# A decoder layer on one Trainium2 core: FFN output sums carried in PSUM by ScalarE, accumulators copied out by ScalarE, and two-chunk plans in blocks 3 and 5

## The chip, the core and the metric

One core of a Trainium2 chip runs the whole kernel. Its engines work side by side, each through a queue of its own in order: TensorE (PE: matmuls, and PEld, its weight loads), VectorE (DVE), ScalarE (ACT), GpSimd (POOL) and SyncE (SP, which here issues the loads of weights). They wait for each other by semaphores. SBUF holds the working data; the matmuls accumulate in PSUM, eight banks of 128 partitions x 512 floats. The metric is the device time of one execution in microseconds (us), the median of several.

## The reference

A decoder layer over 256 tokens of width 2048, all in float32: an FFN, a token mixer (sparse attention beside a recurrence), and a second FFN, each with a residual and a layer norm. The change touches the two FFNs alone:

```python
def swiglu(h, w_in, w_out):
    a, b = jnp.split(h @ w_in, 2, axis=-1)
    return (jax.nn.silu(a) * b) @ w_out

h = layer_norm(DN_ALPHA * h + 0.5 * swiglu(h, ffn1_w_in[l], ffn1_w_out[l]), ln1_g[l], ln1_b[l])
...
h = layer_norm(DN_ALPHA * h + 0.5 * swiglu(h, ffn2_w_in[l], ffn2_w_out[l]), ln3_g[l], ln3_b[l])
```

with 2048 inputs, 2 x 5632 hidden columns and 2048 outputs.

## The kernel before

**Precision.** Each float32 operand is split into a high and a low part, both of a type that TensorE multiplies in one pass, and a product is three matmuls (`three`: high by high, high by low, low by high; L564 to L566). For the weights ScalarE makes the high part (`wh`, L192) and VectorE subtracts it from the weight for the low one (`wl`, L193), piece by piece, up to 1024 columns each. This splitting is most of the two engines' work in the FFNs. Pieces are split four ahead of their use (`AHEAD`) into five pairs of buffers and loaded another four ahead.

**Blocks.** An FFN is 22 blocks. A block computes 256 hidden columns of each of a and b (with the tokens' 256 columns as the moving side, so hidden channels lie on partitions) in two PSUM accumulators `c[0]` and `c[1]`, called `mm` in the trace. There are two such banks in all (`CB`, bufs 2), so the first product of a block into `mm` can't start until the block before has been read out of both. The sum over the 2048 inputs is cut into four chunks. A chunk is computed plainly (form "c": two pieces of 1024 columns, 24 matmuls of 512 columns), or by a scheme with seven products in place of eight on half-size operands (forms `p1q3`, `p2`, `q5p7`, `q4p6`: 42 matmuls of 256 columns). The seven-product form saves TensorE work and needs sums of weights, which VectorE makes (L165, L169, L172) before they are split. Four of its partial sums, p1, p6, p7 and q5, stand in two further banks `e` (`bp` in the trace), and the gate adds them to the accumulators. `layer_plans` says which blocks have how many seven-product chunks (`block_plan(3, 4)`: three chunks, four fills).

**Fills.** The second matmul of the FFN runs in the blocks as fills (form "o"): the hidden blocks are grouped (`SEGS`: 2 blocks, then 4 x 5), and while one group is computed, the outputs of the group before are formed, 4 column ranges `nb` of 512, in two banks `ob` (`OB`, bufs 2), one for each half of the tokens. A range of groups 1 to 4 (`s` is counted from 0) sums over four blocks and is finished with the four fills of one block; in the plan of blocks 6 to 21 two fills come first in the block and two at its end. Group 0 is summed in blocks 2 to 5 with two fills each. At the end of each range VectorE adds half of the bank to the running output `Y` in SBUF (`y_add`, L699). The last group is done after the blocks by `out_product`, which uses `y_add` on its own path.

**The gate.** After a block's last product `gate` puts p1, p6, p7, q5 and the accumulators together into z (SBUF, 4 x 256 columns, one buffer), takes the silu of a, multiplies with b (L871), and 7 pieces later (`LAG_T`) TensorE transposes z back (L877); ScalarE and VectorE split the result into `g` (L689, L690) for the fills. In the code before, ScalarE only copies p1 to z (L859) and takes the silu (L866); VectorE does the adds (L860, L861, L862) and, last, L865 twice: z plus `c[t]`, which reads the accumulators.

**Order.** PE, SP and POOL run in the order in which the code is written. ACT and DVE are put in order by a scheduler at build time, which is free to move an instruction among others where data allows.

Of the kernel before, what the change touches and what calls it, by code (L numbers as in the profile page):

```python
# [8 lines left out]
F32 = mybir.dt.float32  # L9
F32R = mybir.dt.float32r  # L10
I32 = mybir.dt.int32
AF = mybir.ActivationFunctionType
OP = mybir.AluOpType
AX = mybir.AxisListType.X

P = 128
S = 256
# [36 lines left out]
Z_BUFS = 1  # L54
# [12 lines left out]
def block_plan(fast, fills, lead=2):  # L67

    chunks = {0: (), 2: (1, 3), 3: (1, 2, 3)}[fast]
    plain = [("c", k) for q in range(4) if q not in chunks for k in (4 * q, 4 * q + 2)]
    forms = [(f, q) for q in chunks for f in FORMS]
    rest = ["o"] * fills
    plan = [(rest.pop(), 0) for _ in range(min(lead, fills))] + [plain.pop(0)]
    slow = []
    while plain or rest:
        for which in (rest, plain) if lead else (plain, rest):
            if which:  # L80
                p = which.pop(0)
                slow.append((p, 0) if p == "o" else p)
    if not forms:
        return plan + slow
    step = len(forms) / (len(slow) + 1)
    n = 0
    for i, f in enumerate(forms):
        plan.append(f)
        if len(slow) > n and i + 1 >= (n + 1) * step:
            plan.append(slow[n])  # L90
            n += 1
    return plan


def layer_plans(first):
    return ([block_plan(0, 0), block_plan(first, 0)] + [block_plan(2, 2, 0), block_plan(3, 2)] * 2
            + [block_plan(3, 4)] * 16)


# [162 lines left out]
def tile_layer(ctx, tc, x_fm, x_tm, pos, f1a, f1o, wA, wki, wB, lru, wab, wrb, wo, f2a, f2o,  # L262
# [5 lines left out]
    V, A, T, G = nc.vector, nc.scalar, nc.tensor, nc.gpsimd  # L268
    count = [0]

    def name(s):
        count[0] += 1
        return f"{s}{count[0]}"
# [4 lines left out]
    def UHL(s):  # L278
        return U(s, F32R).rearrange("p (a t) -> p a t", a=2)

    def T1(s="t"):
        return pool.tile([P, S], F32, name=name(s), tag="t", bufs=T_BUFS)
# [10 lines left out]
    def OB():  # L293
        return psum.tile([P, 512], F32, name=name("ob"), tag="ob", bufs=2)
# [7 lines left out]
    def BP():  # L302
        return psum.tile([P, 512], F32, name=name("bp"), tag="bp", bufs=4)
# [35 lines left out]
    for i in range(NR + LAG):  # L339
        if i < NR:  # L340
            plain([wB[RX + i], wB[RG + i]])
        if i >= LAG:
            g, c = divmod(i - LAG, TPG)
# [8 lines left out]
    W = Weights(nc, pool, pieces, bg.step)  # L352
# [165 lines left out]
    Y = [[None] * 4 for _ in range(2)]  # L518
# [43 lines left out]
    def three(ps, xh, xl, w, start, stop, seeded=False):  # L562
        h, l = (v.rearrange("p (a h c) -> p a c h", h=2, c=P) for v in w)
        T.matmul(ps, xh, h, start=start, stop=False, skip_group_check=seeded)  # L564
        T.matmul(ps, xh, l, start=False, stop=False, skip_group_check=seeded)  # L565
        T.matmul(ps, xl, h, start=False, stop=stop, skip_group_check=seeded)  # L566

    def tokens(ps, x, t, w, start, stop, seeded=False):
        three(ps, x[:, 0, t * P:(t + 1) * P], x[:, 1, t * P:(t + 1) * P], w, start, stop, seeded)
# [118 lines left out]
    def split(dst, f):  # L688
        A.activation(dst[:, 0], f, AF.Copy)  # L689
        V.tensor_tensor(dst[:, 1], f, dst[:, 0], op=OP.subtract)  # L690
# [3 lines left out]
    def new_stats():  # L694
        stats["st"] = [pool.tile([P, 24], F32, name=name("st"), tag="st", bufs=2) for _ in range(2)]

    def y_add(ps, nb, stat, t):
        y = Y[t][nb]
        V.scalar_tensor_tensor(y, ps[t], 0.5, y, op0=OP.mult, op1=OP.add)  # L699
        if stat:  # L700
            V.bn_stats(stats["st"][t][:, nb * 6:nb * 6 + 6], y)
# [149 lines left out]
    def ffn(x, forms, ln, plans):  # L851
        def gate(c, e, g, i, lag):

            z = W.fast_pool.tile([P, 4 * S], F32, name=name("z"), tag="z", bufs=Z_BUFS)
            z4 = z.rearrange("p (j c) -> p j c", j=4)
            a, b = z4[:, 0:4:2], z4[:, 1:4:2]
            if e:
                p1, p6, p7, q5 = e[0][:, :S], e[0][:, S:], e[1][:, :S], e[1][:, S:]
                A.activation(z4[:, 0], p1, AF.Copy)  # L859
                V.tensor_tensor(z4[:, 1], z4[:, 0], p6, op=OP.add)  # L860
                V.tensor_tensor(z4[:, 2], z4[:, 1], p7, op=OP.add)  # L861
                V.tensor_tensor(b, q5[:, None, :].to_broadcast([P, 2, S]), z4[:, 1:3], op=OP.subtract)  # L862
                for t in range(2):
                    zt = z[:, t * 512:(t + 1) * 512]
                    V.tensor_tensor(zt, zt, c[t], op=OP.add)  # L865
                A.activation(a, a, AF.Silu)  # L866
            else:
                for t in range(2):
                    A.activation(z4[:, 2 * t], c[t][:, :S], AF.Silu)
                    A.activation(z4[:, 2 * t + 1], c[t][:, S:], AF.Copy)  # L870
            V.tensor_tensor(a, a, b, op=OP.mult)  # L871
            for _ in range(lag):
                yield
            ps = BP()
            for k in range(2):
                for t in range(2):
                    T.transpose(ps[:, k * S + t * P:k * S + (t + 1) * P], z[:, t * 512 + k * P:t * 512 + (k + 1) * P], ident)  # L877
            for k in range(2):
                hl = UHL("g")
                split(hl, ps[:, k * S:(k + 1) * S])  # L880
                g[i + k] = hl

        g = [[None] * (2 * (b1 - b0)) for b0, b1 in SEGS]
        fills = deque(FILLS)
        open_ps = []

        def seed():
            s, nb, _ = fills[0]
            open_ps[:] = OB(), OB()

        def fill():
            if not open_ps:
                seed()
            s, nb, k0 = fills.popleft()
            for k in (k0, k0 + 1):
                w = W.unit(512)
                for t in range(2):
                    tokens(open_ps[t], g[s][k], t, w, k == 0, k == len(g[s]) - 1)
            if k0 + 2 == len(g[s]):
                for t in range(2):  # L900
                    y_add(open_ps, nb, False, t)
                if fills:
                    seed()

        for s, (b0, b1) in enumerate(SEGS):
            for n in range(b0, b1):
                c, e = blockF(x, forms, plans[n], fill)
                task = gate(c, e, g[s], 2 * (n - b0), LAG_T[n == NBK - 1])
                next(task)
                bg.add("gate", task)  # L910
        new_stats()
        ln.prepare()
        if not ln.last:
            bg.add("main", later(consts(), W.last.ins))
        out_product(g[-1], ln)
# [189 lines left out]
    for j in range(NK):  # L1105
        s = sumB(blockB(hs))
# [6 lines left out]
    for j in range(NK):  # L1113
        s = sumB(blockB(ya))
# [40 lines left out]
    for j in range(NR + LAG):  # L1155
        if j < NR:
            s = block3(hs)
# [12 lines left out]
        if j >= LAG:  # L1170
            i = j - LAG
            g, c = divmod(i, TPG)
# [6 lines left out]
            r, t = T1(), T1()  # L1179
# [11 lines left out]
    for j in range(NK):  # L1191
        s = sumB(blockB(hs))
# [8 lines left out]
    for j in range(NK):  # L1201
        s = sumB(blockB(yr))
# [91 lines left out]
```

## Time and profile before

| what | us |
|---|---|
| median of 3 runs (2427.35 to 2430.88) | 2427.51 |
| profiled execution, its own time | 2428.93 |
| span of that execution in the trace | 2427.0 |
| PE busy (share of span) | 2313.7 (95%) |
| PEld busy | 2104.2 (87%) |
| DVE busy | 2038.9 (84%) |
| ACT busy | 1410.3 (58%) |
| mean granted TensorE clock | 0.987 of full |

The first FFN lasts from the start to some 710 us, the mixer to some 1690, the second FFN to the end. A busy share is an average over these stages; what a stage is worth is read from the stage. In rows of the timeline the columns are start, duration, engine, line of the code, operation, output<-inputs, shape, and in brackets the idle time before and what ended it. In groups (by line) they are busy time and mean of one in ns, then the idle time in front. Rows of waits read: engine and line that waited, for which engine and line; total, times, longest. Matmuls overlap, so the distance from one start to the next is a matmul's cost, not its duration. "issue" is time in which the engine waited for nothing that the profile shows.

### The profile page before, as it was taken

To read this page: it belongs to the slowest core of one execution; us is meant where nothing else is said; L and a number is where in the kernel's file an instruction comes from. 1 tells how busy PE (TensorE), PEld (TensorE's weight loads), DVE (VectorE), ACT (ScalarE), POOL (GpSimd) and SP (SyncE) were. 2 spreads that over 40 slices of the span, in tenths; PEclk is the share of its full clock that TensorE was granted. 3 is DMA by queue.
4 is the path that set the end of the run, shared out by engine and by line. 5 is a ranking of instruction groups with operands and counts; after the bars stand their busy time and mean duration, and the time that the engine had idled before them with its cause. 6 is when DMAs were issued, how large, how long until landed. Compare 5 with 4: busy or idle time off the path is not lost.

```text
span 2427.0 us, 37550 instructions
## 1 busy us (share of the span) xinstructions
PE 2313.7 (95%) x14592; PEld 2104.2 (87%) x14592; DVE 2038.9 (84%) x2835; ACT 1410.3 (58%) x1931; POOL 25.9 (1%) x58
## 2 busy tenths in 40 slices
PE   7889999999989999999999999999989999999997
PEld 6788888888878888888999988888878888888886
DVE  7889999999987776655788875666989999999996
ACT  6555655655646555544688874444755655655652
POOL 0000000000000000000000000000000000000001
PEclk9999999999999999999999999999999999999998
DMA  7445555555556554455555555556645555556563
GB/s 285 167 171 195 208 198 197 193 193 194 197 178 213 180 177 156 148 183 189 176 190 183 182 198 185 187 192 194 213 172 203 193 189 199 197 207 222 208 215 111
DMA packets 112770, 463.41 MB, mean 191 GB/s; under 512 B 12720, under 2 KB 12720, under 8 KB 97488
## 3 DMA queue, kind: packets, MB, share of 16 engines
q1 hardware_dynamic: 110592, 454.61, 53.6%
q0 software_dynamic: 2000, 6.41, 1.0%
q8 instruction: 114, 1.87, 0.3%
q14 instruction: 64, 0.52, 0.1%
HBM read 458.87 MB, written 2.10 MB: 190 GB/s over the span
## 4 chain that ended last, share of the span: by engine, by line
PE 83%; DVE 8%; issue 5%; ACT 3%; DMA 1%; POOL 0%; DVEq 0%; SPq 0%; ACTq 0%; POOLq 0%
PE mm L564 8%; PE mm L566 8%; PE mm L565 8%; PE ob L564 6%; PE ob L566 6%; PE ob L565 6%; PE mm L553 5%; PE ob L553 5%; PE bp L566 4%; PE bp L565 4%; PE bp L564 4%; DVE wl L193 3%; PE mm L554 3%; PE ob L554 3%; ACT wh L192 2%
## 5 line engine op out<-in xcount | busy, mean ns | idle before, releaser
L193 DVE TENSOR_TENSOR wl<-raw,wh 128x1024 fp32r<-128x1024 f32 (+3 forms) x630 | 752.7, 1202 | 300.8 <-ACT wh L192 300.3
L192 ACT ACTIVATE wh<-raw 128x1024 fp32r<-128x1024 f32 (+3 forms) x630 | 652.8, 1045 | 502.7 <-issue 146.3
L192 ACT ACTIVATE wh<-rf 128x1024 fp32r<-128x1024 f32 x354 | 320.5, 916 | 181.6 <-PE mm L566 143.9
L193 DVE TENSOR_TENSOR wl<-rf,wh 128x1024 fp32r<-128x1024 f32 x354 | 365.9, 1041 | 10.6 <-ACT wh L192 7.0
L564 PE MATMUL ob<-wh,g 128*128 128x512 f32 x640 | 246.6, 385 | 1.0 <-ACT g L689 1.0
L566 PE MATMUL ob<-wh,g 128*128 128x512 f32 x640 | 243.2, 380 | 0.6 <-DVE g L690 0.6
L565 PE MATMUL ob<-wl,g 128*128 128x512 f32 x640 | 243.1, 380 | 0.0
L564 PE MATMUL mm<-wh,hs 128*128 128x512 f32 (+1 forms) x600 | 207.5, 346 | 30.0 <-ACT wh L192 15.7
L192 ACT ACTIVATE wh<-ws 128x1024 fp32r<-128x1024 f32 x118 | 125.3, 1061 | 146.2 <-issue 62.9
L566 PE MATMUL mm<-wh,hs 128*128 128x512 f32 (+1 forms) x600 | 205.0, 342 | 1.7 <-DVE hs L755 1.4
L565 PE MATMUL mm<-wl,hs 128*128 128x512 f32 (+1 forms) x600 | 204.6, 341 | 0.0
L564 PE MATMUL mm<-wh,xs 128*128 128x256 f32 (+1 forms) x464 | 156.6, 338 | 46.2 <-ACT wh L192 24.5
L565 PE MATMUL bp<-wl,sh 128*128 128x256 f32 x708 | 195.1, 276 | 1.6 <-DVE wl L193 1.6
L566 PE MATMUL bp<-wh,sl 128*128 128x256 f32 x708 | 194.7, 275 | 0.0
L564 PE MATMUL bp<-wh,sh 128*128 128x256 f32 x708 | 194.6, 275 | 0.0
L564 PEld LDWEIGHTS mm<-wh,hs 128*128 128x128 f32 x600 | 114.6, 191 | 48.3 <-ACT wh L192 22.6
L565 PE MATMUL mm<-wl,xs 128*128 128x256 f32 (+1 forms) x464 | 154.2, 332 | 1.3 <-DVE wl L193 1.3
L193 DVE TENSOR_TENSOR wl<-ws,wh 128x1024 fp32r<-128x1024 f32 x118 | 144.0, 1221 | 13.1 <-ACT wh L192 13.1
L566 PE MATMUL mm<-wh,xs 128*128 128x256 f32 (+1 forms) x464 | 154.2, 332 | 0.0
L165 DVE TENSOR_TENSOR ws<-rf 128x1024 f32<-128x1024 f32 x118 | 143.8, 1219 | 0.0
L564 PEld LDWEIGHTS mm<-wh,xs 128*128 128x128 f32 x464 | 90.4, 195 | 60.6 <-ACT wh L192 30.5
L565 PEld LDWEIGHTS bp<-wl,sh 128*128 128x128 f32 x708 | 135.8, 192 | 3.6 <-DVE wl L193 2.4
(301 smaller groups left out, 5795.3 us busy)
## 6 DMA issues: line engine op xcount, KB each, us to landing
raw<-wB SPq DMA_DIRECT2D x144, 512.0 KB, 3.6
rf<-f1a SPq DMA_DIRECT2D x60, 1024.0 KB, 4.8
rf<-f2a SPq DMA_DIRECT2D x58, 1024.0 KB, 4.9
raw<-f1o SPq DMA_DIRECT2D x88, 512.0 KB, 5.7
raw<-f2o SPq DMA_DIRECT2D x88, 512.0 KB, 5.7
raw<-wA SPq DMA_DIRECT2D x64, 512.0 KB, 3.6
raw<-f2a SPq DMA_DIRECT2D x60, 512.0 KB, 4.9
raw<-f1a SPq DMA_DIRECT2D x56, 512.0 KB, 5.7
```

Of the source, the lines that this page charges most:

```text
L165: v.tensor_tensor(t, b[:, 0:4:3], b[:, 1:2].to_broadcast([P, 2, 2, 256]), op=OP.add)
L192: nc.scalar.activation(hp, src, AF.Copy)
L193: self.last = nc.vector.tensor_tensor(lp, src, hp, op=OP.subtract)
L553: T.matmul(ps, w[0], x.rearrange("p a t -> p (a t)"), start=first, stop=False)
L554: T.matmul(ps[:, :S], w[1], x[:, 0], start=False, stop=last)
L564: T.matmul(ps, xh, h, start=start, stop=False, skip_group_check=seeded)
L565: T.matmul(ps, xh, l, start=False, stop=False, skip_group_check=seeded)
L566: T.matmul(ps, xl, h, start=False, stop=stop, skip_group_check=seeded)
```

## The change

Three edits, all in the FFNs:

1. `layer_plans`: blocks 3 and 5 have two seven-product chunks in place of three, as blocks 2 and 4 have.
2. `gate`: z has 6 x 256 columns. ScalarE copies both accumulators and p1 into z (new L860 twice, L861) at the block's end, so that the accumulators are read by ScalarE alone. VectorE then adds p1, p6, p7, q5 and the copies (L862 to L867: four of 256 columns and two of 512) from what is now mostly SBUF; silu is L868, the product L873.
3. `seed` and `fill`: for the groups s = 1 to 4 ScalarE writes 2 x Y into the bank `ob` before the first fill (L893), the fills' matmuls add to it from the first one on (start false), and at the range's end ScalarE copies the bank out to Y with scale 0.5 (L906). VectorE's two `y_add` of such a range go. Group 0 keeps them.

```diff
--- before.py
+++ after.py
@@ -93,7 +93,7 @@
 
 
 def layer_plans(first):
-    return ([block_plan(0, 0), block_plan(first, 0)] + [block_plan(2, 2, 0), block_plan(3, 2)] * 2
+    return ([block_plan(0, 0), block_plan(first, 0)] + [block_plan(2, 2, 0), block_plan(2, 2)] * 2
             + [block_plan(3, 4)] * 16)
 
 
@@ -851,23 +851,25 @@
     def ffn(x, forms, ln, plans):
         def gate(c, e, g, i, lag):
 
-            z = W.fast_pool.tile([P, 4 * S], F32, name=name("z"), tag="z", bufs=Z_BUFS)
-            z4 = z.rearrange("p (j c) -> p j c", j=4)
-            a, b = z4[:, 0:4:2], z4[:, 1:4:2]
+            z = W.fast_pool.tile([P, 6 * S], F32, name=name("z"), tag="z", bufs=Z_BUFS)
+            z6 = z.rearrange("p (j c) -> p j c", j=6)
+            a, b = z6[:, 0:4:2], z6[:, 1:4:2]
             if e:
                 p1, p6, p7, q5 = e[0][:, :S], e[0][:, S:], e[1][:, :S], e[1][:, S:]
-                A.activation(z4[:, 0], p1, AF.Copy)
-                V.tensor_tensor(z4[:, 1], z4[:, 0], p6, op=OP.add)
-                V.tensor_tensor(z4[:, 2], z4[:, 1], p7, op=OP.add)
-                V.tensor_tensor(b, q5[:, None, :].to_broadcast([P, 2, S]), z4[:, 1:3], op=OP.subtract)
                 for t in range(2):
-                    zt = z[:, t * 512:(t + 1) * 512]
-                    V.tensor_tensor(zt, zt, c[t], op=OP.add)
+                    A.activation(z6[:, 2 * t:5 + t:4 - t], c[t].rearrange("p (j c) -> p j c", j=2), AF.Copy)
+                A.activation(z6[:, 1], p1, AF.Copy)
+                V.tensor_tensor(z6[:, 0], z6[:, 0], p1, op=OP.add)
+                V.tensor_tensor(z6[:, 1], z6[:, 1], p6, op=OP.add)
+                V.tensor_tensor(z6[:, 3], z6[:, 1], p7, op=OP.add)
+                V.tensor_tensor(z6[:, 2], z6[:, 2], z6[:, 3], op=OP.add)
+                V.tensor_tensor(b, q5[:, None, :].to_broadcast([P, 2, S]), b, op=OP.subtract)
+                V.tensor_tensor(b, b, z6[:, 4:6], op=OP.add)
                 A.activation(a, a, AF.Silu)
             else:
                 for t in range(2):
-                    A.activation(z4[:, 2 * t], c[t][:, :S], AF.Silu)
-                    A.activation(z4[:, 2 * t + 1], c[t][:, S:], AF.Copy)
+                    A.activation(z6[:, 2 * t], c[t][:, :S], AF.Silu)
+                    A.activation(z6[:, 2 * t + 1], c[t][:, S:], AF.Copy)
             V.tensor_tensor(a, a, b, op=OP.mult)
             for _ in range(lag):
                 yield
@@ -887,6 +889,8 @@
         def seed():
             s, nb, _ = fills[0]
             open_ps[:] = OB(), OB()
+            for t in range(2 if s else 0):
+                A.activation(open_ps[t], Y[t][nb], AF.Copy, scale=2.0)
 
         def fill():
             if not open_ps:
@@ -895,10 +899,13 @@
             for k in (k0, k0 + 1):
                 w = W.unit(512)
                 for t in range(2):
-                    tokens(open_ps[t], g[s][k], t, w, k == 0, k == len(g[s]) - 1)
+                    tokens(open_ps[t], g[s][k], t, w, not s and k == 0, k == len(g[s]) - 1, bool(s))
             if k0 + 2 == len(g[s]):
                 for t in range(2):
-                    y_add(open_ps, nb, False, t)
+                    if s:
+                        A.activation(Y[t][nb], open_ps[t], AF.Copy, scale=0.5)
+                    else:
+                        y_add(open_ps, nb, False, t)
                 if fills:
                     seed()
```

What a scheduler made of it is seen in the built programs' orders, in three places. In these rows each line is the code line, operation, output<-inputs with buffer numbers, and shape.

First, ScalarE at the end of a late block (6 to 21). Before, the last splits of the old block (`wh` of `raw` and `rf`) stand directly ahead of the gate's copy of p1:

```order
L192 ACTIVATE wh_3335<-raw_3261 128x1024
L192 ACTIVATE wh_3355<-raw_3279 128x1024
L192 ACTIVATE wh_3367<-raw_3298 128x1024
L192 ACTIVATE wh_3383<-rf_3317 128x1024
L859 ACTIVATE z_3401<-bp_3138 128x256
L192 ACTIVATE wh_3412<-rf_3317 128x512
L192 ACTIVATE wh_3429<-ws_3385 128x1024
L192 ACTIVATE wh_3450<-raw_3365 128x1024
```

With the change:

```order
L192 ACTIVATE wh_3316<-raw_3242 128x1024
L906 ACTIVATE y_318<-ob_3001 128x512
L893 ACTIVATE ob_3334<-y_349 128x512
L906 ACTIVATE y_320<-ob_3002 128x512
L192 ACTIVATE wh_3338<-raw_3260 128x1024
L893 ACTIVATE ob_3335<-y_351 128x512
L192 ACTIVATE wh_3350<-raw_3279 128x1024
L192 ACTIVATE wh_3366<-rf_3298 128x1024
L860 ACTIVATE z_3384<-mm_3099 128x2x256
L860 ACTIVATE z_3384<-mm_3100 128x2x256
L861 ACTIVATE z_3384<-bp_3119 128x256
L192 ACTIVATE wh_3398<-rf_3298 128x512
```

Two copies out of `ob` (L906) and the first one into the next pair of banks (L893) now stand ahead of the split `wh_3338` (`wh_3355` before), the second one behind it. The two accumulator copies (L860) stand after the old block's last splits, ahead of the copy of p1, which is L861 now.

Second, VectorE at the same place. Before (two L699 stand three rows above the first of these):

```order
L193 TENSOR_TENSOR wl_3368<-raw_3298,wh_3367 128x1024
L193 TENSOR_TENSOR wl_3384<-rf_3317,wh_3383 128x1024
L860 TENSOR_TENSOR z_3401<-z_3401,bp_3138 128x256
L169 TENSOR_TENSOR rf_3317<-ws_3385,rf_3317 128x2x256
L861 TENSOR_TENSOR z_3401<-z_3401,bp_3139 128x256
L193 TENSOR_TENSOR wl_3413<-rf_3317,wh_3412 128x512
L862 TENSOR_TENSOR z_3401<-bp_3139,z_3401 128x2x256
L172 TENSOR_TENSOR rf_3317<-rf_3317 128x2x256
L865 TENSOR_TENSOR z_3401<-z_3401,mm_3118 128x512
L865 TENSOR_TENSOR z_3401<-z_3401,mm_3119 128x512
L193 TENSOR_TENSOR wl_3430<-ws_3385,wh_3429 128x1024
L871 TENSOR_TENSOR z_3401<-z_3401 128x2x256
```

With the change, from the gate's first add on:

```order
L862 TENSOR_TENSOR z_3384<-z_3384,bp_3119 128x256
L863 TENSOR_TENSOR z_3384<-z_3384,bp_3119 128x256
L193 TENSOR_TENSOR wl_3399<-rf_3298,wh_3398 128x512
L864 TENSOR_TENSOR z_3384<-z_3384,bp_3120 128x256
L172 TENSOR_TENSOR rf_3298<-rf_3298 128x2x256
L865 TENSOR_TENSOR z_3384<-z_3384 128x256
L193 TENSOR_TENSOR wl_3416<-ws_3368,wh_3415 128x1024
L866 TENSOR_TENSOR z_3384<-bp_3120,z_3384 128x2x256
L193 TENSOR_TENSOR wl_3437<-raw_3348,wh_3436 128x1024
L867 TENSOR_TENSOR z_3384<-z_3384 128x2x256
L165 TENSOR_TENSOR ws_3472<-rf_3396 128x1024
L873 TENSOR_TENSOR z_3384<-z_3384 128x2x256
```

L699 is gone, and the two reads of `mm` (L865) with it; the adds of the gate are spread over more rows, and the product (L871 before, L873 now) stands behind three splits and sums of 1024 columns instead of one.

Third, ScalarE at the boundary from block 3 to block 4, where no fill's bank changes hands in a way that ScalarE sees (group 0). Before:

```order
L192 ACTIVATE wh_1141<-raw_1073 128x1024
L192 ACTIVATE wh_1159<-rf_1087 128x1024
L192 ACTIVATE wh_1171<-rf_1087 128x512
L192 ACTIVATE wh_1190<-raw_1123 128x1024
L859 ACTIVATE z_1206<-bp_980 128x256
L192 ACTIVATE wh_1219<-ws_1161 128x1024
L866 ACTIVATE z_1206<-z_1206 128x2x256
```

With the change:

```order
L192 ACTIVATE wh_1119<-raw_1036 128x1024
L192 ACTIVATE wh_1131<-rf_1066 128x1024
L860 ACTIVATE z_1184<-mm_969 128x2x256
L192 ACTIVATE wh_1149<-rf_1066 128x512
L192 ACTIVATE wh_1168<-raw_1101 128x1024
L860 ACTIVATE z_1184<-mm_970 128x2x256
L861 ACTIVATE z_1184<-bp_988 128x256
L192 ACTIVATE wh_1200<-ws_1133 128x1024
```

The copy of `c[0]` stands ahead of two of the last splits of the block, that of `c[1]` and of p1 behind them.

## The prediction

> **What bounds the kernel now.** I read the page first, its busy shares by slice.
>
> ```profile
> PE   7889999999989999999999999999989999999997
> DVE  7889999999987776655788875666989999999996
> ```
>
> Both FFNs (left third, right third) keep TensorE and VectorE above 90% together; between them TensorE alone is full. The diff touches the FFNs only. Next, windows over their blocks: FFN1's blocks 2 to 7, cut where TensorE begins each.
>
> ```profile
> 58.60:93.02 34.42, 26.90 (x161) 24.58 (x161) 26.80 (x33) 15.65 (x18) 0.00 (x0) 0.90 0.46 164
> 93.02:118.65 25.63, 25.29 (x180) 23.62 (x178) 25.52 (x33) 15.42 (x20) 0.00 (x0) 1.00 0.46 169
> 118.65:154.52 35.87, 26.84 (x161) 24.51 (x161) 28.31 (x34) 16.18 (x19) 0.00 (x0) 0.90 0.48 173
> 154.52:179.99 25.47, 25.13 (x180) 23.66 (x179) 25.36 (x33) 15.25 (x19) 0.00 (x0) 1.00 0.47 170
> 179.99:214.68 34.69, 31.97 (x205) 29.15 (x203) 32.73 (x39) 19.75 (x24) 0.00 (x0) 0.95 0.58 211
> 214.68:246.09 31.41, 30.29 (x205) 28.01 (x204) 30.96 (x38) 18.75 (x22) 0.00 (x0) 1.00 0.53 200
> ```
>
> Columns: window, length, busy of PE, PEld, DVE, ACT, POOL, granted clock. Blocks 2, 4 and 6 are some 9, 10 and 4 us longer than their PE time at full clock; every later block takes 31.41 us, of which DVE fills 30.96. The waits of TensorE name the releaser:
>
> ```profile
> PE mm L564 <- DVE z L865: 40.5, 8, 9.0
> PE mm L564 <- ACT wh L192: 40.2, 31, 6.7
> PE bp L565 <- DVE wl L193: 2.2, 5, 0.6
> ```
>
> The timeline of PE places the long ones, each at the first product of a block into the accumulators `mm`:
>
> ```profile
> 66.12 0.77 PE L564 MATMUL mm<-wh,xs 128*128 128x512 f32 x1 [7.52 <-DVE z L865]
> 127.68 0.77 PE L564 MATMUL mm<-wh,xs 128*128 128x512 f32 x1 [9.03 <-DVE z L865]
> 188.05 0.45 PE L564 MATMUL mm<-wh,xs 128*128 128x512 f32 x1 [2.72 <-DVE z L865]
> 690.74 0.76 PE L564 MATMUL mm<-wh,g 128*128 128x512 f32 x1 [4.78 <-DVE z L865]
> 1803.23 0.77 PE L564 MATMUL mm<-wh,hs 128*128 128x512 f32 x1 [9.03 <-DVE z L865]
> 1863.79 0.45 PE L564 MATMUL mm<-wh,hs 128*128 128x512 f32 x1 [2.71 <-DVE z L865]
> 2366.59 0.77 PE L564 MATMUL mm<-wh,g 128*128 128x512 f32 x1 [3.46 <-DVE z L865]
> ```
>
> The 31 waits on "ACT wh" are the same wait in the late blocks. A late boundary (the last fill's end at 368.37, the next block's `mm` at 378.20), rows of PE, ACT, DVE:
>
> ```profile
> 368.37 0.27 PE L564 MATMUL mm<-wh,xs 128*128 128x256 f32 x1
> 369.04 0.28 PE L564 MATMUL bp<-wh,sh 128*128 128x256 f32 x1
> 376.69 0.38 PE L566 MATMUL ob<-wh,g 128*128 128x512 f32 x1
> 378.20 0.45 PE L564 MATMUL mm<-wh,xs 128*128 128x512 f32 x1 [1.13 <-ACT wh L192]
> 384.21 0.27 PE L877 MATMUL bp<-ident,z 128*128 128x128 f32 x1
> ...
> 368.62 2.04 ACT L192 ACTIVATE wh<-raw 128x1024 fp32r<-128x1024 f32 x2 [1.43 <-issue]
> ...
> 369.69 1.28 DVE L699 SCALAR_TENSOR_TENSOR y<-ob,y 128x512 f32<-128x512 f32 x2
> 370.89 2.35 DVE L193 TENSOR_TENSOR wl<-raw,wh 128x1024 fp32r<-128x1024 f32 x2
> 373.16 1.22 DVE L193 TENSOR_TENSOR wl<-rf,wh 128x1024 fp32r<-128x1024 f32 x1
> 374.30 0.41 DVE L860 TENSOR_TENSOR z<-z,bp 128x256 f32<-128x256 f32 x1
> 374.63 0.68 DVE L169 TENSOR_TENSOR rf<-ws,rf 128x512 f32<-128x512 f32 x1
> 377.37 1.28 DVE L865 TENSOR_TENSOR z<-z,mm 128x512 f32<-128x512 f32 x2
> 378.56 1.22 DVE L193 TENSOR_TENSOR wl<-ws,wh 128x1024 fp32r<-128x1024 f32 x1
> ```
>
> The first L865 ends at 378.05, 0.15 before the matmul, exactly the distance at 188.05 and 690.74; the ACT row is a coincidence. So one thing holds TensorE at every block's end: `mm` is freed by the last adds of a chain on a VectorE that is full.
>
> **Late blocks (6 to 21).** DVE instructions follow each other at 1.14 us for 1024 columns (370.89 to 373.16 for two), 0.60 for 512 and 0.33 for 256 (374.30 to 374.63). Removed: two L699, 1.20. The gate chain was L860, L861, L862, L865 twice (0.33 + 0.33 + 3 x 0.60); it becomes four of 256 and two of 512 (4 x 0.33 + 2 x 0.60), 0.1 more. DVE: 30.96 - 1.2 + 0.1 = 29.85 us. PE without its wait: a matmul of 512 follows the last after 0.215, so 376.69 + 0.215 against 378.20 loses 1.3, and the first piece lasts 2.66 for 2.59 (rows below): 31.41 - 1.36 = 30.05 us. Both are now within 0.2 us, so what is late next decides.
>
> That is ScalarE's queue at the block's end. It gets six copies there: two sums out, two seeds in, two accumulators. Behind them wait three `wh`, then their `wl` on DVE, then the gate. Prices:
>
> ```profile
> L977 ACT ACTIVATE stg<-mm 128x512 f32<-128x512 f32 x8 | 4.8, 597 | 4.7 <-PE mm L566 4.7
> L859 ACT ACTIVATE z<-bp 128x256 f32<-128x256 f32 x41 | 15.6, 382 | 10.2 <-PE bp L566 10.2
> 40.64 1.14 ACT L530 ACTIVATE y<-y 128x512 f32<-128x512 f32 x2
> ```
>
> A PSUM copy of 512 takes 0.60, and the next starts after 0.52 (1.14 for two); a `wh` of 1024 after 0.96. No row shows ScalarE writing PSUM: between a 256 copy (0.38) and a 1024 one (1.06) I take 0.60, that of the same size. The page "ScalarE: Activation LUTs" of the Trainium skill (What ACT_TABLE_LOAD costs; Step-by-step) gives 186 ns + 0.833 ns a column, an estimate of 0.61 us for 512, and calls PSUM the faster destination; by it the sum stays.
>
> From T0 = 368.37 in the old block's terms: sum out at 0.25 (as `wh` at 368.62), the seed waits for its end, 0.9, second sum 1.4, `wh` 1.95, seed 2.9, two `wh` 3.4 and 4.4, accumulators 5.35 and 5.9, `p1` 6.4, done 6.8. DVE: first gate add 6.85, then by its new order 256, 512, 256, 512, 256, 1024, 512, 1024, 512, 1024 columns, and the product: 3 x 0.33 + 0.33 + 4 x 0.60 + 3 x 1.14 = 7.1, starts 14.0, ends 14.7. TensorE wants z for its transposes at 384.21 - 368.37 - 1.36 = 14.5. So **a new wait, on the product (now L873), of about 0.35 us** takes the old one's place: 30.4 us a block. The seeds are in at 3.4; the fill that needs the second one gets there at 3.35 (six-matmul steps of 0.67, rows 368.37 and 369.04, five of them) + 0.65: covered by 0.5. `wl` for the next fill is also ready some 0.2 early. If this cover goes, TensorE stalls by the excess. Gain 1.0 us over 2 x 15 boundaries: **-30 us**; ends: 0 (chain 1 us longer, with seeds at 1.06) and -41 (no wait, 30.05).
>
> **Early blocks.** A long wait costs twice: after it matmuls run slowly.
>
> ```profile
> 66.12:70.25 4.13, 4.13 (x12) 3.43 (x13) 1.74 (x3) 0.63 (x1) 0.00 (x0) 0.64 0.00 0
> 188.05:192.41 4.36, 4.36 (x13) 3.46 (x14) 4.36 (x5) 0.63 (x1) 0.00 (x0) 0.61 0.00 0
> 359.17:361.76 2.59, 2.59 (x14) 2.27 (x13) 2.59 (x3) 1.59 (x2) 0.00 (x0) 1.00 1.03 413
> 378.20:380.86 2.66, 2.66 (x12) 2.31 (x13) 2.66 (x4) 0.64 (x1) 0.00 (x0) 1.00 0.00 0
> ```
>
> The same 12 matmuls take 4.13 and 4.36 after waits of 7.5 and 2.7 us (granted clock 0.64, 0.61), 2.66 after 1.1, and 2.59 undisturbed: 1.5 to 1.8 us on top. The Trainium skill ("TensorE: Matmul & The Clock Gate", What's actually happening) has the clock halved only after an idle window of about 3.4 us; by it the 2.7 us waits would cost nothing more and the sum would be 3.5 us smaller, but the row at 188.05 shows the loss, so it stays.
>
> Accumulator 0 is complete before the last seven-product pieces, accumulator 1 after half of the last one; ScalarE copies both within about 1.2 us of that. Left over: 0.5 us at 66.12, where a `wh` stands between the copies and c1's comes at 59.6, and 0.2 at the two long ones. Then: FFN1 block 1 to 2, 7.5 + 1.5 - 0.5 = 8.5; block 3 to 4 in both FFNs, 2 x (9.0 + 1.5 - 0.2) = 20.6; block 5 to 6 in both, 2 x (2.7 + 1.8) = 9.0. Blocks 3 and 5 give up a seven-product chunk. PE pays 24 matmuls of 512 at 0.215 for 42 of 256 at 0.112 (0.67/6): 0.5 each, 1.9 in all, against which some of the five stalls on `wl` (2.2 us, third row of the waits) go with the VectorE work; I call that even. On DVE such a chunk costs four `wl`, 3 x 1.14 + 0.60, and three sums, 1.14 + 2 x 0.60: 6.4 us. As a plain chunk it costs two `wl`, 2.3 us, so 4.1 less. In the pair of blocks of the third and fourth window DVE has 28.31 + 25.36 = 53.7 to do, PE 26.84 + 25.13 less 1.5 of slow restart, 50.5; with the change it is 49.6 beside 51. DVE then keeps up where PE no longer stands still, and that is what makes the rest of this term real. If it doesn't, half of this term returns. The loads change from one of 1 MB to two of 0.5 MB for such a chunk, same bytes, issued four pieces ahead, DMA 0.46 to 0.58 busy: nothing. Sum **-38 us**.
>
> **Ends of the FFNs.** 690.74 and 2366.59 are the same wait. FFN2: 3.5 + 1.5 (as at 66.12) - 0.4 = 4.6. FFN1: there DVE has constants to compute behind it and is full until the output products, so I count only 2 us, the sums out and adds that it loses. **-6.6 us.**
>
> **Sum.** The profiled execution took 2428.9 us (span 2427.0), 1.4 over the median. 2428.9 - 30 - 38 - 6.6 = **2354.3**; with the block model good to no better than a microsecond I say 2355.
>
> **Rivals.**
> A: ScalarE's chain eats the late gain (each seed near 1.06, or the copies reached 1 us late). It is for this that six copies wait for a fill's end ahead of three `wh`; against it, ACT is busy 18.75 of 31.41. 2428.9 - 44 (the other two terms) = 2385.
> B: no new wait; two engines at 99%. The margins of 0.2 to 0.5 speak against it. 2428.9 - 41 - 38 - 6.6 = 2343.
> C: late blocks as said, but DVE lags in blocks 2 to 6 and half of that term returns: 2354.3 + 19 = 2373.
> D: the change doesn't do what it says, since ScalarE, in order, reaches the accumulators no sooner than VectorE did: the early waits stay and DVE's savings alone count, some 10 us: 2419. The order above speaks against it.
> E: slower. The cycle fill, sum out, seed, `wh`, `wl`, gate, transposes, next fill sets the block. It costs 30.4 with copies of 0.60. The early and end gains are 44 us; 30 blocks must lose more than that, 1.5 us each over 31.41, so 32.9: the chain 2.5 us longer, six copies at about 1.02 or both seeds at 1.85. From there on it is slower; at 1.1 each it is 2428.9 - 44 + 30 x 2 = 2445. Every PSUM row of ACT is at 0.60 or less.
>
> **Chances.** Forecast 0.50 (2348 to 2362), A 0.17, B 0.13, C 0.12, D 0.04, E 0.04. The range takes in A to C with the seed's bounds: 2340 to 2387. A measurement of this kernel tells about 0.2% (5 us) from no change. Faster 0.95, same 0.01, slower 0.04.
>
> **What would show it.** In the changed profile: no PE wait on DVE's z adds into `mm`; clock 1.00 through 66 to 215 us; late blocks of 30.4 us with DVE still above 97% and a short wait at the transposes on L873; seed rows (ACT, ob<-y) near 0.60; TensorE's first `ob` matmul not waiting. Wrong if blocks stay at 31.4 with DVE idle on "ACT wh" behind the copies (A), or if PE waits on `wl` in blocks 2 to 6 (C).

## The result, and the profile after

The changed kernel takes 2334.08 us (median of 4, 2333.59 to 2336.85) against 2427.43 (median of 4): a ratio of 0.9615, with a 95% interval of 0.9598 to 0.9631. That is faster by 93 us, where 72 were forecast, and below the range (2340 to 2387). The profiled execution took 2333.59, 95.3 less than the one before.

The page of the changed kernel, its busy shares by slice (40 slices of the span):

```profile
PE   8999999999999999999999999999999999999996
DVE  8999999999987786555788875665999999999997
PEclk9999999999999999999999999999999999999999
```

TensorE is now above 90% in every slice but the first and the last. Windows over blocks 2 to 5 of FFN1 and over one late block, columns as in the prediction (length, then busy of PE, PEld, DVE, ACT, POOL, granted clock):

```profile
57.00:171.00 114.00, 114.00 (x720) 104.93 (x720) 113.36 (x144) 74.04 (x93) 0.00 (x0) 1.00 0.55 196
350.60:380.65 30.05, 30.05 (x204) 28.12 (x203) 29.88 (x37) 21.47 (x28) 0.00 (x0) 1.00 0.55 210
```

In 114 us of the early blocks TensorE does not stand still once and its clock stays at 1.00. A late block takes 30.05 us, all of it TensorE's, with 29.88 of VectorE beside it. What is left of the waits of TensorE, the four largest over the whole run:

```profile
PE mm L564 <- ACT wh L192: 7.0, 2, 6.2
PE mm L564 <- ACT z L872: 3.5, 2, 2.4
PE bp L972 <- DVE stg L955: 1.9, 1, 1.9
PE bp L879 <- DVE z L873: 1.5, 1, 1.5
```

The 6.2 us are the first matmul of the program. The transposes (L879) waited for the product (L873) a single time, in the last block of FFN2; the prediction had them wait in each of 30 late blocks. New operations, by line:

```profile
L860 ACT ACTIVATE z<-mm 128x512 f32<-128x512 f32 x82 | 44.8, 588 | 6.6 <-PE mm L566 6.6
L893 ACT ACTIVATE ob<-y 128x512 f32<-128x512 f32 x64 | 38.2, 596 | 3.5 <-DVE y L699 2.6
L906 ACT ACTIVATE y<-ob 128x512 f32<-128x512 f32 x64 | 37.6, 588 | 6.6 <-PE ob L566 6.5
```

A seed, ScalarE writing 512 columns of PSUM, takes 0.596 us, a copy out 0.588: the 0.60 that the prediction took for both.

Where the time went is read from the first transpose of z of a block, which the timeline of PE shows in every kernel. Z0, Z5 and Z20 are the transposes of the first, sixth and twenty-first block of an FFN. For FFN1, Z0, Z5 and Z20 before and after:

```profile
46.18 0.49 PE L877 MATMUL bp<-ident,z 128*128 128x128 f32 x3
195.75 0.49 PE L877 MATMUL bp<-ident,z 128*128 128x128 f32 x3
666.87 0.38 PE L877 MATMUL bp<-ident,z 128*128 128x128 f32 x2
```

```profile
45.45 0.38 PE L879 MATMUL bp<-ident,z 128*128 128x128 f32 x2
170.32 0.49 PE L879 MATMUL bp<-ident,z 128*128 128x128 f32 x3
621.02 0.49 PE L879 MATMUL bp<-ident,z 128*128 128x128 f32 x3
```

Z0 to Z5 is 149.57 before and 124.87 after, Z5 to Z20 471.12 and 450.70. The stages of both FFNs together, the same way for the parts taken one by one (us; "ends" is, in FFN1, Z20 to the first matmul of L553, which stands in the mixer, at 790.69 before, and in FFN2 Z20 to the end of the last matmul):

| kernel | early, Z0 to Z5 | late, Z5 to Z20 | ends |
|---|---|---|---|
| before | 284.4 | 942.4 | 192.4 |
| plans alone (plans_alone) | 270.4 | 947.2 | 191.2 |
| gate alone (gate_alone) | 251.0 | 930.7 | 184.2 |
| sums alone (sums_alone) | 284.8 | 964.1 | 194.9 |
| plans and sums, gate of before (old_gate) | 270.7 | 961.8 | 193.3 |
| plans and gate, `y_add` kept (old_sums) | 243.4 | 928.9 | 184.8 |
| gate and sums, three chunks kept (old_plans) | 252.1 | 904.2 | 177.8 |
| all three: the changed kernel | 243.4 | 901.4 | 179.6 |

So the changed kernel gains 41.0 in the early blocks, 41.0 in the late ones, 12.8 at the ends; another 0.7 stands ahead of FFN1's Z0. The ends differ by up to 1.8 us between kernels that differ in the plans alone, which do not touch them, so differences of that size there say nothing.

### The profile page after: what moved, and what is told of

The parts are those of the page before. It is cut to its first block, busy times and chain, and to the rows that moved or that the text cites. A ratio compares the mean times of both kernels' runs of the same rounds, so it can differ in the third digit from the quotient of the medians.

```text
span 2331.8 us, 37449 instructions
## 1 busy us (share of the span) xinstructions
PE 2293.7 (98%) x14520; PEld 2097.9 (90%) x14520; DVE 1987.6 (85%) x2792; ACT 1501.8 (64%) x2133; POOL 25.9 (1%) x58
## 4 chain that ended last, share of the span: by engine, by line
PE 91%; issue 4%; DVE 2%; ACT 1%; DMA 1%; POOL 0%; SPq 0%; DVEq 0%; ACTq 0%; POOLq 0%
PE mm L566 9%; PE mm L564 9%; PE mm L565 9%; PE ob L564 7%; PE ob L566 7%; PE ob L565 7%; PE mm L553 6%; PE ob L553 5%; PE bp L566 4%; PE bp L565 4%; PE bp L564 4%; PE mm L554 3%; PE ob L554 3%; PE mm L1151 2%; PE ob L1151 2%
## 5 line engine op out<-in xcount | busy, mean ns | idle before, releaser
L193 DVE TENSOR_TENSOR wl<-raw,wh 128x1024 fp32r<-128x1024 f32 (+2 forms) x638 | 765.1, 1202 | 274.5 <-ACT wh L192 271.4
L192 ACT ACTIVATE wh<-raw 128x1024 fp32r<-128x1024 f32 (+2 forms) x638 | 663.6, 1044 | 409.3 <-PE mm L566 107.2
L192 ACT ACTIVATE wh<-rf 128x1024 fp32r<-128x1024 f32 x342 | 307.0, 915 | 150.0 <-PE mm L566 93.4
L193 DVE TENSOR_TENSOR wl<-rf,wh 128x1024 fp32r<-128x1024 f32 x342 | 352.6, 1040 | 4.3 <-ACT wh L192 2.0
L565 PE MATMUL bp<-wl,sh 128*128 128x256 f32 x684 | 188.1, 275 | 0.0
L566 PE MATMUL bp<-wh,sl 128*128 128x256 f32 x684 | 188.1, 275 | 0.0
L564 PE MATMUL mm<-wh,xs 128*128 128x512 f32 (+1 forms) x472 | 157.0, 333 | 9.4 <-ACT wh L192 7.0
L565 PE MATMUL mm<-wl,xs 128*128 128x512 f32 (+1 forms) x472 | 156.5, 332 | 1.3 <-DVE wl L193 1.3
L566 PE MATMUL mm<-wh,xs 128*128 128x512 f32 (+1 forms) x472 | 156.3, 331 | 0.0
L566 PEld LDWEIGHTS ob<-wh,g 128*128 128x128 f32 x640 | 121.2, 189 | 17.5 <-DVE g L690 0.3
L564 PEld LDWEIGHTS ob<-wh,g 128*128 128x128 f32 x640 | 121.5, 190 | 15.2 <-ACT g L689 0.9
L565 PEld LDWEIGHTS ob<-wl,g 128*128 128x128 f32 x640 | 121.6, 190 | 14.3
```

The lines of the kernel that those rows point to most:

```text
L192: nc.scalar.activation(hp, src, AF.Copy)
L193: self.last = nc.vector.tensor_tensor(lp, src, hp, op=OP.subtract)
```

## The experiments

Thirteen kernels ran. Times are medians of four or more executions, each with the ratio to the kernel before on the same chip at the same time; those medians of before lie between 2428.2 and 2429.6.

### One part undone

The changed kernel with one edit taken back: the gate's code of before; `y_add` (L699) in place of seed and copy out; `block_plan(3, 2)` for blocks 3 and 5. A part of the second:

```diff
-                A.activation(open_ps[t], Y[t][nb], AF.Copy, scale=2.0)
...
-                    if s:
-                        A.activation(Y[t][nb], open_ps[t], AF.Copy, scale=0.5)
-                    else:
-                        y_add(open_ps, nb, False, t)
+                    y_add(open_ps, nb, False, t)
```

> The changed kernel with the gate of before (VectorE reads the accumulators again); sums in PSUM and two-chunk plans stay. Theory: the early waits and those at the FFNs' ends came from VectorE freeing the accumulators, so they return, shortened where the plans take 4.1 us of VectorE work per block: some 25 us early and 8 at the ends; late blocks have less VectorE work than before (no y_add), so they stay within 0.5 us of 30.05. 2334 + 33 = 2367, up to 2380. Rival: VectorE's load alone made the waits, and the plans and sums have cured that: 2334 to 2340.

> The changed kernel with VectorE's y_add in place of the sums carried in PSUM. Theory: late blocks become bound by VectorE again, 29.85 + 1.2 = 31.05 us against 30.05 for TensorE, so 30 x 1.0 to 1.1 more: 2364 to 2367; the waits at the accumulators do not return, since ScalarE frees them. Rival: the accumulators' copies alone set the late block, and VectorE's work is absorbed by its run-ahead: 2334.

> The changed kernel with three seven-product chunks in blocks 3 and 5 again. Theory: VectorE has 53.7 us for a pair of blocks against 50.5 of TensorE, so it falls behind by some 3 us a pair where ScalarE no longer lets TensorE wait at the accumulators: four pairs, 2334 + 12 = 2346, with TensorE waiting on wl. Rival: the gate alone removed the early waits and VectorE's lag is made up inside the wait-free blocks: 2332 (TensorE 1.9 us less).

Measured: old_gate 2433.32 us (ratio 1.0021, 1.0011 to 1.0031); old_sums 2367.51 (0.9748, 0.9733 to 0.9762); old_plans 2342.84 (0.9648, 0.9634 to 0.9663).

The last two came as the theory said. With `y_add` a late block is bound by VectorE again, 31.01 us in place of 30.05, with VectorE busy for 30.93 of them. With three chunks VectorE falls behind in the early blocks, 8.7 us in all, and TensorE waits for `wl` (5.3 us in 8 waits).

The first was a miss by 53 us, and it says most. Without the new gate the other two edits together bring nothing: the early blocks gain 13.7 us and the late ones lose 19.4. A late block and one of its starts, kernel with the old gate, window and timeline:

```profile
376.77:408.81 32.04, 30.27 (x202) 27.98 (x203) 30.27 (x36) 20.74 (x26) 0.00 (x0) 1.00 0.53 198
```

```profile
408.81 0.46 PE L564 MATMUL mm<-wh,xs 128*128 128x512 f32 x1 [1.78 <-DVE z L865]
```

VectorE is busy for 0.7 us less than before (30.27 for 30.96) and the block is 0.65 us longer. It stands idle for 1.77 us, behind ScalarE. I had counted VectorE's work; what sets the accumulators' release is a chain: ScalarE's copies out and seeds, then the splits, then `wl`, then the gate's adds, the last of which reads `mm`. The sums on ScalarE lengthen that chain by four copies. This is read from the order and the rows; no run with the old gate took the copies alone off that chain.

### One part alone

The same three edits, each alone on the kernel before.

> The kernel before with only the two-chunk plans in blocks 3 and 5. Theory, after the run with the old gate: its blocks 2 to 5 are the same as here, and they took 5.2 and 6.2 us less than before; the late blocks are untouched. 2428 - 11 = 2417. Rival: the plans are what makes the early waits go, 2428 - 38 = 2390.

> The kernel before with only the new gate. Theory: early and end waits go, less the 8.8 us that the three-chunk plans cost; late blocks bound by VectorE at 31.0 in place of 31.41 (as in the run with y_add): 2367.5 + 8.8 = 2376. Rival: the edits only work together, as the sums with the old gate did: 2428 or more.

> The kernel before with only the sums carried in PSUM. Theory, after the run with the old gate: ScalarE's four copies stand ahead of the splits that the gate's adds wait behind on VectorE, so VectorE frees the accumulators 0.8 us later though it has less to do; late blocks of 32.06 against 31.41, 30 x 0.65 = 19.5 us more: 2448. Rival: the loss with the old gate came from the new plans' blocks; 1.2 us of VectorE a block saved gives 2428 - 30 = 2398.

Measured: plans_alone 2416.41 (0.9948, 0.9933 to 0.9963); gate_alone 2375.38 (0.9781, 0.9765 to 0.9797); sums_alone 2451.73 (1.0093, 1.0077 to 1.0110).

All three totals came near the theory, reformed after the old gate, that of plans_alone by two misses that nearly cancel: its early blocks gained 14.0 us where 11 were expected, and its late ones, expected untouched, lost 4.8 (the first late block of each FFN takes 32.41 us, one in FFN2 34.15). Why they lost that is not settled. The sums alone are a loss of 22 us and, behind the new gate, a gain: 2367.51 without them, 2334.08 with them, 33 us. In the table the late stage shows it: sums alone +21.7, gate alone -11.7, the two together -38.2 (old_plans), with the plans -41.0. Each cures what limits the other: the new gate takes VectorE out of the accumulators' release but leaves VectorE full at 31.0 us; the sums take 1.2 us off VectorE but put four copies ahead of the release, which no longer holds the release back once ScalarE itself does it.

### Does ScalarE's chain have room?

The prediction said that a wait for the product would take the old wait's place. It did not come. The chain in the changed kernel, one late boundary; the last products of the fill on PE, then ACT, then DVE, then the transposes:

```profile
365.54 0.38 PE L564 MATMUL ob<-wh,g 128*128 128x512 f32 x1
365.75 0.38 PE L565 MATMUL ob<-wl,g 128*128 128x512 f32 x1
365.97 0.38 PE L566 MATMUL ob<-wh,g 128*128 128x512 f32 x1
...
380.65 0.60 PE L879 MATMUL bp<-ident,z 128*128 128x128 f32 x4
```

```profile
365.74 0.60 ACT L906 ACTIVATE y<-ob 128x512 f32<-128x512 f32 x1 [0.19 <-PE ob L566]
366.36 0.60 ACT L893 ACTIVATE ob<-y 128x512 f32<-128x512 f32 x1
366.90 0.58 ACT L906 ACTIVATE y<-ob 128x512 f32<-128x512 f32 x1
367.38 1.05 ACT L192 ACTIVATE wh<-raw 128x1024 fp32r<-128x1024 f32 x1
...
370.76 1.06 ACT L860 ACTIVATE z<-mm 128x512 f32<-128x512 f32 x2
371.71 0.38 ACT L861 ACTIVATE z<-bp 128x256 f32<-128x256 f32 x1
```

```profile
372.23 0.41 DVE L862 TENSOR_TENSOR z<-z,bp 128x256 f32<-128x256 f32 x1
...
379.43 0.68 DVE L873 TENSOR_TENSOR z<-z 128x512 f32<-128x512 f32 x1
```

In the prediction's terms T0, the end of the last fill, is 365.97 + 0.215 = 366.18. The first copy out starts 0.45 us ahead of T0, not 0.25 behind it: the three rows shown are bank 1's products, and bank 0 was complete 3 x 0.215 earlier. The product ends at 380.11, T0 + 13.9; the transposes are due at T0 + 14.5.

First, two kernels with ScalarE work added: each accumulator copied to z twice, and the first sum of a range copied out twice.

```diff
-                for t in range(2):
+                for t in (0, 0, 1, 1):
                     A.activation(z6[:, 2 * t:5 + t:4 - t], c[t].rearrange("p (j c) -> p j c", j=2), AF.Copy)
```

```diff
-                        A.activation(Y[t][nb], open_ps[t], AF.Copy, scale=0.5)
+                        for _ in range(2 - t):
+                            A.activation(Y[t][nb], open_ps[t], AF.Copy, scale=0.5)
```

> The changed kernel in which ScalarE copies each accumulator out twice in the gate: 1.04 us more of ScalarE work between the last split of a block and the gate's first add. Theory: the product ends 0.4 to 0.5 us before TensorE wants it in the late blocks, so 1.04 us more (and the scheduler's move of some 0.5 us of VectorE work in front of the product) make TensorE wait about 1.0 us a block at the transposes: 30 x 1.0, 2364. Rival: the chain through ScalarE has some us of room and TensorE alone sets the block: 2334.

> The changed kernel in which ScalarE copies the first of a range's two sums out twice: 0.52 to 0.6 us more at the head of the chain to the product, with VectorE's order as it was. The prediction had the first copy start 0.25 us after the last fill; the changed kernel's trace has it 0.45 us before. Theory: those 0.7 us are the room in which no wait shows, and of them some 0.6 are left at the transposes (1.04 us of copies and 0.48 of moved VectorE work cost 0.92 a block), so this extra copy costs nothing or up to 0.1 us a block: 2334 to 2338. Rival: there is no room left, and each 0.5 us of ScalarE work costs its own time: 30 x 0.5, 2349.

Measured: copies_twice 2367.94 (0.9748, 0.9734 to 0.9763); sum_out_twice 2343.60 (0.9648, 0.9634 to 0.9662). The waits of TensorE in the first:

```profile
PE bp L879 <- DVE z L873: 22.5, 31, 1.1
```

There is the wait that was forecast, at the place that was forecast, in 31 blocks; a late block takes 30.96 us. The second comes out between its two theories. Its product and its transposes:

```profile
380.59 0.68 DVE L873 TENSOR_TENSOR z<-z 128x512 f32<-128x512 f32 x1
...
381.33 0.66 PE L879 MATMUL bp<-ident,z 128*128 128x128 f32 x4
```

T0 is 366.61 there. The product ends 14.66 us after it, and the transposes start at once, at T0 + 14.72 in place of 14.47; a late block takes 30.36 us, which is the prediction's 30.4. So there was some room, but less than 0.5 us.

Next, the head start alone, with no instruction more. In one kernel the last products of a range alternate between the banks, in the other all six of bank 0 come first.

```diff
+                    for i, j, r in ((0, h, False), (0, l, False), (1, h, True)):
+                        for t in range(2):
+                            T.matmul(open_ps[t], g[s][k][:, i, t * P:(t + 1) * P], j, start=False, stop=r,
...
```

```diff
+            if s and k0 + 2 == len(g[s]):
+                order = [(t, k) for t in range(2) for k in (k0, k0 + 1)]
...
```

early_and_twice is the second of these with each accumulator copied twice.

> The changed kernel in which the last three products of the two sums of a range alternate between the banks, so that both sums are complete at nearly the same time and the first copy out starts 0.2 us before the last fill's end in place of 0.45 (no instruction more or less; the scheduler now puts both seeds ahead of the first split). Theory: what the prediction missed is this head start; without it VectorE, whose 29.85 us leave 0.2 of 30.05, waits for the splits: 30.2 to 30.4 us a late block, 2340 to 2345. Rival: the head start plays no part, the product had room anyway: 2334 to 2336.

> The changed kernel in which the last fill of a range does all six products of the first bank, then all six of the second: the first copy out can start some 0.65 us earlier still. Theory: TensorE alone sets the late block now (30.05 us without a wait), so nothing is gained: 2333 to 2336. Rival: ScalarE's chain still costs something in the late blocks: 2320 to 2330.

> The last two ideas of the earlier runs together: the first bank's products first, and each accumulator copied twice. Theory: the earlier first copy takes about one copy of 0.5 us off the head of ScalarE's chain (the second copy out still waits for the last product), so of the 0.92 us a block that the double copies cost 0.4 to 0.5 are left: 30.5 us a block, 2347 to 2351. Rival: the double copies cost through something else (VectorE's moved work, the accumulators' release), and the 0.92 stay: 2364 to 2368.

Measured: banks_together 2335.55 (0.9615, 0.9601 to 0.9629); bank0_first 2347.27 (0.9668, 0.9654 to 0.9683); early_and_twice 2351.78 (0.9684, 0.9668 to 0.9700).

banks_together missed its theory: the head start is gone (first copy at T0 - 0.02), the product ends 0.43 us later, and nothing is lost. Product and transposes in that kernel:

```profile
380.80 0.68 DVE L873 TENSOR_TENSOR z<-z 128x512 f32<-128x512 f32 x1
...
381.61 0.60 PE L879 MATMUL bp<-ident,z 128*128 128x128 f32 x4
```

The product ends at 381.48, 0.13 us ahead of the transposes, which stand at T0 + 14.47 as in the changed kernel. So the room of the changed kernel is those 0.43 us, used up here to the last tenth; the theory that VectorE, waiting for the splits, would lengthen the block was wrong. early_and_twice came as expected, 30.48 us a block in place of 30.96.

bank0_first cannot be read as a test of the head start, since the scheduler changed another thing with it: the second of VectorE's two `g` splits (L690) now stands ahead of a `wl`, and ScalarE's `wh` behind both of its own. VectorE of that kernel:

```profile
357.41 0.42 DVE L690 TENSOR_TENSOR g<-bp,g 128x256 fp32r<-128x256 f32 x1
358.29 1.23 DVE L193 TENSOR_TENSOR wl<-ws,wh 128x1024 fp32r<-128x1024 f32 x1 [0.46 <-ACT wh L192]
```

It idles there for 0.46 us in every late block. With 29.9 of work in 30.05, that much cannot be made up: after two or three blocks of 30.05 us the product comes too late, the transposes wait for it (8.3 us in 25 waits), and a block takes 30.50. Whether a longer head start by itself would cost or gain anything was not shown.

That left two readings of what the copies cost: the product comes too late for the transposes, or VectorE's idle time behind ScalarE (0.78 us a block in copies_twice) is the loss itself. The last two kernels move the transposes back by two pieces, with and without the double copies.

```diff
-LAG_T = (7, 4)
+LAG_T = (9, 4)
```

> The kernel with the accumulators copied twice, and z transposed nine pieces after a block's end in place of seven (some 2 us later, the orders of ScalarE and VectorE around the product unchanged). Theory: the 0.92 us a block that the double copies cost are paid at the transposes, which the product reaches too late; with the later place VectorE may lag and its idle time behind the splits closes, so the block falls to VectorE's own 30.17 us or little over: 30.2 to 30.3, 2338 to 2342. Rival: VectorE's idle time behind ScalarE's copies (0.79 us a block) is itself the loss, wherever the transposes stand: 30.9, 2362 to 2367.

> The changed kernel with z transposed nine pieces after a block's end in place of seven, nothing else. Theory: no late block waits at the transposes now, TensorE sets the block with 30.05: 2332 to 2337. Rival: the place of the transposes still costs (or the later g makes the next fills wait): 5 us or more off.

Measured: twice_later_T 2342.90 (0.9647, 0.9630 to 0.9663), later_T 2337.38 (0.9625, 0.9610 to 0.9639). Z5 to Z20 of FFN1 takes 450.70 us in both, the same as in the changed kernel, where the double copies with the early transposes took 464.49. A late block of copies_twice and one of twice_later_T, windows:

```profile
350.00:380.96 30.96, 30.26 (x203) 28.14 (x203) 30.18 (x37) 22.65 (x31) 0.00 (x0) 1.00 0.55 205
```

```profile
292.34:322.41 30.07, 30.07 (x204) 28.14 (x203) 29.93 (x37) 22.37 (x31) 0.00 (x0) 1.00 0.57 210
```

The loss was paid at the transposes, and VectorE's idle time was its consequence: 30.96 - 30.18 = 0.78 us a block with the early transposes, 0.14 with the late ones. later_T is 0.4 us and twice_later_T 1 us above what was expected; as to the latter, its late blocks are better than expected (30.05 to 30.1), and the other microseconds lie outside them, among them 2.3 in FFN2's late stage, in a few longer blocks. Neither kernel beats the changed one.

## Why the prediction was wrong

**What bounded the kernel** was read rightly: `mm` was freed by the last adds on VectorE, and gate_alone shows that taking those off the path removes the waits.

**Late blocks** (forecast -30, measured -41.0). The step that failed is the start of ScalarE's chain: "sum out at 0.25 (as `wh` at 368.62)". It was taken from a `wh` whose idle time the row puts down to "issue", not to the end of a fill, and it treats the two banks as finished together. Measured, the first copy starts at T0 - 0.45. Of the 0.7 us between, the banks' order is 0.43 and the wrong row the rest; banks_together, which loses the 0.43 alone, was still in time, so it took both to put a wait on paper. Every other link held: first copy to the gate's first add 6.6 by the prediction and 6.49 measured (365.74 to 372.23), first add to product 7.15 and 7.20, need of the transposes T0 + 14.5 and 14.47, seeds 0.60 and 0.596. (The 0.52 from copy to copy came from a row of copies within SBUF; two copies out of PSUM stand 0.48 us apart.) With the head 0.7 us too late, the product ended at 14.7 on paper and at 13.9 on the chip, and on the two sides of 14.4 lie a wait of 0.35 and none. banks_together places that edge (an end of 14.34 is free), sum_out_twice what lies behind it (an end of 14.66 makes a block of 30.36). A margin of 0.2 us was argued from links that were good to half a microsecond; the block without a wait, 30.05 us, was computed exactly and was rival B, to which the text gave 0.13.

**Early blocks** (-38, measured -41.0). Right in mechanism, 3 us too small. The left-over waits of 0.5 and 0.2 us did not come at all: the window of 114 us above has none; that is 0.9 us. The five waits were also put in with the idle time that the rows list, where the late blocks' term had counted from start to start (a wait of 1.13 cost 1.30 there); that is another 0.8. The rest is not settled. The parts are right too: the gate alone gives 33.4 of it, the plans 7.5 more behind it, as the working had them make the rest of the term real (C's condition): with three chunks, VectorE lags.

**Ends** (-6.6, measured -12.8). FFN2: 4.6 forecast, 4.9 measured (Z20 to the end 68.56 and 63.65 us). FFN1: 2 forecast, 7.9 measured (123.82 and 115.93). The step that failed is "DVE has constants to compute behind it and is full until the output products, so I count only 2 us". TensorE's waits there, before and after:

```profile
690.74 0.76 PE L564 MATMUL mm<-wh,g 128*128 128x512 f32 x1 [4.78 <-DVE z L865]
701.64 0.48 PE L564 MATMUL mm<-wh,g 128*128 128x512 f32 x1 [0.98 <-ACT g L689]
704.61 0.80 PE L566 MATMUL mm<-wh,g 128*128 128x512 f32 x1 [2.26 <-DVE g L690]
```

```profile
640.77 0.48 PE L564 MATMUL mm<-wh,g 128*128 128x512 f32 x1 [0.66 <-ACT z L860]
650.23 0.48 PE L564 MATMUL mm<-wh,g 128*128 128x512 f32 x1 [0.98 <-ACT g L689]
651.85 0.56 PE L566 MATMUL mm<-wh,g 128*128 128x512 f32 x1 [0.92 <-DVE g L690]
```

The longest of these waits was for the accumulators, like anywhere else, and ScalarE frees them however full VectorE is. The waits shrink by 5.5 us. The rest is slow matmuls: those behind the first wait go, which the forecast had counted at FFN2's end (1.5 us) and not here, and behind the later two the clock stands at half for 3.41 us (652.13 to 655.54) in place of 6.82 (703.98 to 710.80). This last part is partly chance: in old_plans the same two waits left the clock at full speed. gate_alone has 5.8 us of the 7.9.

**Rivals.** B came, with its late term to a microsecond; its 2343 was 9 us too high by the early term and the ends, which all cases shared, and so the range ended above the result. A, C and D did not come. Slower than before were sums_alone and, by 5 us, old_gate: there a chain through ScalarE got longer, as in E, but it ended at the release of the accumulators, which still hung on VectorE, and not at the transposes.

## What to carry to other kernels

Price a block by its chain as well as by each engine's sum: the sums in PSUM cut VectorE's work, yet alone they cost 22 us, because they lengthened the chain to the release that TensorE waited for. Before two edits are judged one by one, ask which limit each leaves behind; here gate and sums together were worth 38 us in the late blocks, the gate alone 12 and the sums alone minus 22. Where the forecast turns on a margin of a few tenths, take every link from the row of the very instruction, such as which bank's last matmul releases the copy, or let the range take in both sides.

## What the runs showed of the hardware

TensorE's clock after a wait. The length of one wait does not settle whether the matmuls behind it run slowly. With the old gate every late block had a wait of some 1.77 us, and the clock stayed at full speed. At FFN1's start a wait of 2.41 us in the changed kernel was followed by slow matmuls, and one of 2.47 us at the same place in later_T was not. At FFN1's end the same two waits of 0.98 and 0.92 us were followed by half clock in the changed kernel and not in old_plans. Windows behind the wait of 1.78 us (old gate), of 2.41 (changed kernel) and of 2.47 (later_T), then from the end of the wait of 0.98 in the changed kernel and in old_plans; the third number from the end is the granted clock:

```profile
408.81:412.50 3.69, 3.69 (x22) 3.34 (x23) 3.66 (x5) 1.46 (x2) 0.00 (x0) 1.00 0.00 0
```

```profile
33.79:37.79 4.00, 4.00 (x11) 3.22 (x12) 3.24 (x7) 1.44 (x3) 0.00 (x0) 0.57 1.02 405
```

```profile
34.72:38.72 4.00, 4.00 (x24) 3.67 (x25) 3.24 (x7) 2.50 (x5) 0.00 (x0) 1.00 1.03 409
```

```profile
650.23:654.23 4.00, 3.08 (x8) 2.09 (x9) 3.24 (x16) 0.50 (x2) 0.00 (x0) 0.74 0.73 239
```

```profile
656.44:660.44 4.00, 3.08 (x12) 2.11 (x13) 3.93 (x19) 0.66 (x3) 0.00 (x0) 1.00 0.70 233
```

No edge between a harmless and a harmful length comes out of these rows, and what else decides is not shown. The Trainium skill ("TensorE: Matmul & The Clock Gate", What's actually happening) has the clock halved after an idle window of about 3.4 us. The waits of 2.41, 0.98 and 0.92 us are all shorter, so these rows do not bear that out as the least length of a wait; the measured rows decide. ScalarE writes 512 columns of PSUM in 0.596 us and copies as many out in 0.588, so a copy costs nearly the same in either direction here; copies of 512 within SBUF (L530, before the change) took 0.62.
